# A decoder trunk on one core: where the operands of the matmuls lie in SBUF, modulo 256 bytes

## The chip, the core and the metric

The kernel runs on one core of one Trainium2 chip. The metric is device time in microseconds, from one execution of the whole program; the median of the runs is compared.

## What is computed

A trunk of two layers works on 256 tokens of 1024 channels, in float32. Cut to what matters:

```python
for l in range(2):
    h = h + 0.5 * rmsnorm(swiglu(rmsnorm(h, g[0]), w_gu[l, 0], w_down[l, 0]), g[1])   # FFN, width 2816
    z = rmsnorm(h, g[2]) @ w_in[l]                     # 1024 -> 9224 columns
    y_m = mlstm(conv(z_qk), z_v, z_i, z_f) * sigmoid(z_o)
    y_s = spatial_gating(gelu(z_u), gelu(z_sv), ...)
    y_x = cross_attention(z_xq, rmsnorm(mem, g[6]) @ w_mkv[l])
    merged = sum(sigmoid(z_g)[b] * (y_b @ w_branch[l, b]) for b, y_b in enumerate((y_m, y_s, y_x)))
    h = h + rmsnorm(merged @ w_out[l], g[3])
    h = h + 0.5 * rmsnorm(swiglu(rmsnorm(h, g[4]), w_gu[l, 1], w_down[l, 1]), g[5])
```

## The kernel before, in words

Every large product is done with float32 operands split in two, a high part rounded to the type fp32r and a low part that is the rest; a product is then three matmuls, high by high, high by low, low by high (`product`, L180 to 186, and `rows_mm`, L198 to 205). A matmul has a stationary operand, which a load of its own puts into the array (the profile's PEld), and a moving operand, which streams through (in the profile's `out<-in` the moving operand is named first). Two shapes carry nearly all of the work.

- **256 columns** (L185): the stationary operand is a 128x128 block of a weight, the moving operand one of the eight 256-token rows of an activation. This is `pair_T`: 48 matmuls make 256 output channels. It does the gate and up projections of the FFNs (`o<-xh,hi`, `o<-xh,lo`, `o<-xl,hi`), most of w_in, the three branch projections (`yxh`, `yxl`, `ymh`, `yml`, `ysh`, `ysl`), and the keys of the memory (`mh`, `ml`). Also of this shape are the scores of the cross-attention (`so_<-kT,qx`, the queries stationary) and `attend` (`o<-pT,vx`, the values stationary).
- **512 columns** (L203 to 205): the stationary operand is a 128x128 block of an activation, the moving operand 512 columns of a weight. This is the down projection of the FFNs (`acc<-hi,hh`), the value and spatial parts of w_in (`o<-hi,xh`), the values of the memory (`o<-hi,mh`) and w_out (`acc<-hi,mth`).

One FFN runs over 11 steps; a step is two `pair_T` (96 matmuls of 256 columns) and then, for two slices of the step before, 24 matmuls of 512 columns. A mixer layer is a chain of such groups with short pieces of softmax, scan and normalisation between them. Weights come through a ring: SP issues a DMA into `raw` (4 buffers), ScalarE casts it to `hi` (6 buffers, L114), VectorE subtracts to give `lo` (6 buffers, L115). The order of work on each engine is that of the program text, with a few explicit "issue after" edges (`behind`); the change touches none of them.

Where a tile lies is set by the order of the text. Pools follow one another (`const`, `stream`, `act`, `tmp`, `small`), inside a pool the tags stand in the order of their first use, each at the size of its largest tile times its number of buffers, rounded up to 32 bytes. The first pool starts at byte 16512 of each partition. Summing the sizes gives these starts, modulo 256: `raw`, `hi`, `lo` and all tiles of the tags `t2` and `cv` 192; `xh` 192 and `xl` 0, `qk` 64, `vm` 128, `kT` 192, `ymh` 192, `vx` 0, `yml` 0, `yxh` 64, `yxl` 128. Inside these, `placed` (L118) makes an activation 64 bytes wider than needed and starts it at a given element: 8 (32 bytes) for most, 0 for `mth` and `mtl`, and a value for each of the six FFNs and mixers for `xh` and `xl` (`X_AT`, L37). Every other step inside these operands is a multiple of 512 bytes (blocks of a weight) or 1024 bytes (rows of an activation), so a pair of tiles has one distance modulo 256 for all of its matmuls.

The distance of a pair, moving minus stationary, modulo 256, comes out so (the first number is for the high part of the activation, the second for the low part):

```
256 columns                       moving - stationary
FFN 0 of layer 0   X_AT 4           16,  80
mixer of layer 0   X_AT 8           32,  96
FFN 1 of layer 0   X_AT 12          48, 112
FFN 0 of layer 1   X_AT 2            8,  72
mixer of layer 1   X_AT 6           24,  88
FFN 1 of layer 1   X_AT 10          40, 104
branches: ym 32, 96   ys 160, 224   yx 160, 224      memory keys (mh, ml): 160, 224
scores (kT, qx): 0                attend (pT, vx): 192
512 columns
FFN down (hi or lo with hh, hl): 0
w_in, layer 0: 224, 160    w_in, layer 1: 232, 168
memory values: 96, 32      w_out: 128, 64
```

Of the kernel before, what the change touches and what calls it, by code (L numbers as in the profile page):

```python
# [8 lines left out]
F32 = mybir.dt.float32  # L9
F32R = mybir.dt.float32r  # L10
# [4 lines left out]
P = 128  # L15
D = 1024
KT = D // P
S = 256
NT = S // P
DEPTH = 2  # L20
NH = 4
DQK = 128
DV = 256
# [9 lines left out]
FREE = 4  # L33
BARE_TAIL = 3
BARE_FREE = 3
LINE = 16
X_AT = {(0, 0): 4, (0, 2): 8, (0, 4): 12, (1, 0): 2, (1, 2): 6, (1, 4): 10}  # L37
C_QK, C_V, C_O, C_I, C_F, C_U, C_SV, C_XQ, C_G = 0, 1024, 2048, 3072, 3076, 3080, 4104, 5128, 6152


# [1 line left out]
def decoder_trunk(ctx: ExitStack, tc: tile.TileContext, x, mem, norm_g, w_ffn_gu, w_ffn_down, w_in, conv_w,  # L42
# [4 lines left out]
    const = ctx.enter_context(tc.tile_pool(name="const", bufs=1))  # L47
    stream = ctx.enter_context(tc.tile_pool(name="stream", bufs=4))
    act = ctx.enter_context(tc.tile_pool(name="act", bufs=1))
    tmp = ctx.enter_context(tc.tile_pool(name="tmp", bufs=2))  # L50
# [2 lines left out]
    psa = ctx.enter_context(tc.tile_pool(name="psa", bufs=4, space=bass.MemoryType.PSUM))  # L53

    h = const.tile([P, NT, D], F32, name="h")
    rowA = tmp.tile([112, P], F32, name="rowA", tag="cv", bufs=3)
    nc.scalar.dma_start(rowA, norm_g.rearrange("l n (k p) -> (l n k) p", p=P))
    for tt in range(NT):
# [19 lines left out]
    nc.gpsimd.tensor_copy(sel, sel_f)  # L78
    ones = const.tile([P, P], F32, name="ones")
    nc.gpsimd.memset(ones, 1.0)  # L80
    mhalf = const.tile([P, LINE], F32, name="mhalf")[:, 0:1]
    nc.gpsimd.memset(mhalf, -0.5)
    junk = const.tile([P, 512], mybir.dt.bfloat16, name="junk")
    colA = const.tile([P, 112], F32, name="colA")
    colB = const.tile([P, P], F32, name="colB")
    mgh = const.tile([P, 16], F32, name="mgh")
    def load_consts(src, dst, n):
        pt = ps.tile([P, 512], F32, name="pt", tag="mm")
        nc.tensor.transpose(out=pt[:, :n], in_=src, identity=ident[:n, :n])
        nc.vector.tensor_copy(dst, pt[:, :n])  # L90

    def g_col(l, n, k):
        i = (l * 7 + n) * 8 + k
        return colA[:, i:i + 1]
# [20 lines left out]
            nc.vector.tensor_tensor(out=lo, in0=raw, in1=hi.bitcast(F32), op=ALU.subtract)  # L115
        return hi, lo

    def placed(name, tag, at):  # L118
        t = act.tile([P, KT * S + LINE], F32R, name=name, tag=tag)
        return t[:, at:at + KT * S].rearrange("p (k s) -> p k s", s=S)  # L120

    def load_cols(w, c0, n):
        his, los = [], []
# [41 lines left out]
    def scaled_split(src, gain, hi, lo):  # L165
        last["act"] = nc.scalar.mul(hi, src, gain)  # L166
        last["dve"] = nc.vector.scalar_tensor_tensor(out=lo, in0=src, scalar=gain, in1=hi.bitcast(F32), op0=ALU.mult,  # L167
                                       op1=ALU.subtract)

    def split(src, hi, lo):  # L170
        nc.scalar.copy(hi, src)  # L171
        nc.vector.tensor_tensor(out=lo, in0=src, in1=hi.bitcast(F32), op=ALU.subtract)  # L172

    def split_x(l, n, pts):
        xh, xl = (placed(name, name, X_AT[l, n]) for name in ("xh", "xl"))
        for kt in range(KT):
            scaled_split(pts[kt // 2][:, kt % 2, :], g_col(l, n, kt), xh[:, kt, :], xl[:, kt, :])
        return xh, xl
# [12 lines left out]
    def pair_T(w, c0, xt):  # L191
        wt = load_cols(w, c0, 2 * P)
        o = ps.tile([P, 2, S], F32, name="o", tag="mm")
        for m in range(2):
            cols_T(o[:, m, :], wt, m * P, xt)
        return o
# [10 lines left out]
    def group_rows(w, c0, xt, qs=range(4), os_=None):  # L207
        os_ = os_ or [ps.tile([P, 512], F32, name="o", tag="mm") for _ in range(NT)]
        for q in qs:
            wt = load_rows(w, q * 2 * P, 2, c0, 512)  # L210
            for k in range(2):
                kt = 2 * q + k
                for tt in range(NT):
                    rows_mm(os_[tt], xt, kt, tt, wt, k, 0, kt == 0, kt == KT - 1)
        return os_
# [19 lines left out]
    def boundary(accs, gb, mul, nxt, fill=(), lead=0):  # L235
# [28 lines left out]
        if lead:  # L264
            pts = new_pts()
            for tt in range(NT):
                transpose_in(xs[tt], tt, pts)
        xt = split_x(*nxt, pts)
        if not lead:
            hold[:] = [[]] * BARE_FREE + [[last["act"], last["dve"]]]  # L270
# [63 lines left out]
    kv = {}  # L334

    def kv_parts(l):
        def start():
            mh, ml = placed("mh", "qk", 8), placed("ml", "vm", 8)
            for kt in range(KT):
                scaled_split(memT[:, kt, :], g_col(l, 6, kt), mh[:, kt, :], ml[:, kt, :])  # L340
            kv[l] = ((mh, ml), [act.tile([P, KT, S], F32R, name="kT", tag=t) for t in ("kT", "ymh")],
                     [act.tile([P, NT, D], F32R, name="vx", tag=t) for t in ("vx", "yml")])

        def k_part(c):
            mt, kT, vx = kv[l]
            o = pair_T(w_mkv[l], c * 2 * P, mt)
            split(o, kT[0][:, 2 * c:2 * c + 2, :], kT[1][:, 2 * c:2 * c + 2, :])

        os_ = {}

        def v_quarter(c, q):
            mt, kT, vx = kv[l]
            os_[c] = group_rows(w_mkv[l], D + c * 512, mt, (q,), os_.get(c))
            if q == 3:
                for tt, o in enumerate(os_[c]):
                    split(o, vx[0][:, tt, c * 512:(c + 1) * 512], vx[1][:, tt, c * 512:(c + 1) * 512])

        return start, ([lambda c=c: k_part(c) for c in range(4)] +
                       [lambda c=c, q=q: v_quarter(c, q) for c in range(2) for q in range(4)])

    def mixer(l, xt, nxt, start=None, fill=(), lead=0):
# [20 lines left out]
        wsT = tmp.tile([P, 4, P], F32, name="wsT", tag="wsT", bufs=1)  # L382
        for g in range(4):
            nc.vector.tensor_tensor(out=wsT[:, g, :], in0=wsp[:, g, :], in1=upper, op=ALU.mult)
        yx = placed("yxh", "yxh", 8), placed("yxl", "yxl", 8)
        sc = DH ** -0.5

        _, kT, vx = kv[l]
# [34 lines left out]
            sl = slice(2 * hd, 2 * hd + 2)  # L423
            split(o, yx[0][:, sl, :], yx[1][:, sl, :])

        vm = act.tile([P, NT, NH, DV + 1], F32, name="vm", tag="vm")
        nc.gpsimd.memset(vm[:, :, :, DV:DV + 1], 1.0)

        def proj_v(c):
# [68 lines left out]
        qk = act.tile([P, KT, S], F32, name="qk", tag="qk")  # L498
# [36 lines left out]
                nc.vector.scalar_tensor_tensor(out=mt[1][:, sl, :], in0=mg[:, sl, :], scalar=0.5,  # L535
                                               in1=mt[0][:, sl, :].bitcast(F32), op0=ALU.mult, op1=ALU.subtract)

        ym = placed("ymh", "ymh", 8), placed("yml", "yml", 8)

        def out_gate(hd):  # L540
            so = tmp.tile([P, 2, S], F32, name="so", tag="t2", bufs=T2)
# [71 lines left out]
            gated(c, yr, so)  # L613

        vn = act.tile([P, NT, D], F32, name="vn", tag="vx")
        ys = placed("ysh", "qk", 8), placed("ysl", "vm", 8)
        for c in range(2):
            for tt, o in enumerate(group_rows(w, C_SV + c * 512, xt)):
                nc.scalar.activation(vn[:, tt, c * 512:(c + 1) * 512], o, AF.Gelu_apprx_tanh)
# [17 lines left out]
        def sgu(g):  # L637
            uT = tmp.tile([P, 2, S], F32, name="uT", tag="t2", bufs=T2)
            nc.scalar.activation(uT, pair_T(w, C_U + g * 2 * P, xt), AF.Gelu_apprx_tanh)
            mx = psa.tile([P, 2, NT, P], F32, name="mx", tag="acc")  # L640
            rb = tmp.tile([P, 2, P], F32, name="rb", tag="cv", bufs=3)
            for m in range(2):
                f = 2 * g + m
                for c in range(NT):
                    nc.tensor.matmul(mx[:, m, c, :], vn[:, c, f * P:(f + 1) * P], wsT[:, g, :], start=True,  # L645
                                     stop=True)
            yf = tmp.tile([P, 2, S], F32, name="yf", tag="t2", bufs=T2)
            for m in range(2):
                f = 2 * g + m
                nc.vector.scalar_tensor_tensor(out=rb[:, m, :], in0=rw[:, g, :], scalar=b_col(112 + l * 8 + f),  # L650
                                               in1=bs[:, g, :], op0=ALU.mult, op1=ALU.add)
                nc.vector.scalar_tensor_tensor(
                    out=yf[:, m, :].rearrange("p (c t) -> p c t", c=NT), in0=mx[:, m], scalar=b_col(96 + l * 8 + f),
                    in1=rb[:, m:m + 1, :].to_broadcast([P, NT, P]), op0=ALU.mult, op1=ALU.add)
            sl = slice(2 * g, 2 * g + 2)
            nc.vector.tensor_tensor(out=yf, in0=yf, in1=uT, op=ALU.mult)
            split(yf, ys[0][:, sl, :], ys[1][:, sl, :])
# [3 lines left out]
        for c in range(4):  # L661
            branch(1, 0, ym, c, gate(0, c))
            sgu(c)
        mt = placed("mth", "yxh", 0), placed("mtl", "yxl", 0)
        for c in range(4):
            branch(2, 1, ys, c, gate(1, c), mt)
        if start:
# [16 lines left out]
    transpose_in(xs, 1, pts)  # L684
    load_consts(rowA, colA, 112)
    xt = split_x(0, 0, pts)
    hold[:] = [[first], [], [last["act"], last["dve"]]]
    xt = ffn(0, 0, xt, (0, 2), {2: load_mem, 4: transpose_mem, 6: start0}, kv0, 3)
    xt = mixer(0, xt, (0, 4), start1, kv1[:3], 2)
    xt = ffn(0, 1, xt, (1, 0), {}, kv1[3:8], 3)  # L690
    xt = ffn(1, 0, xt, (1, 2), {}, kv1[8:], 3)
    xt = mixer(1, xt, (1, 4))
    ffn(1, 1, xt, None)

# [26 lines left out]
```

## Time and profile before

| | |
|---|---|
| median of 3 runs | 1532.0 us (1531.25 to 1532.78) |
| the profiled execution | 1531.97 us, span of its instructions 1530.3 us |
| TensorE matmuls busy | 1511.3 us, 99% |
| TensorE weight loads busy | 1425.0 us, 93% |
| VectorE, ScalarE, GpSimd busy | 930.2, 749.6, 44.7 us |
| matmuls | 10870 |
| mean granted TensorE clock | 0.997 |

A matmul's record (281 to 284 ns for 256 columns in the page's list) is its way through the array, and records of neighbours overlap. What a matmul costs in a stream is the distance from one start or end to the next. It is read here from the chain of work that ended last, where a piece `x96` is 96 matmuls in a row with the time that they took together, and from the starts in the timeline.

### The profile page before, as it was taken

The numbers are of one execution on the slowest core, as the hardware profiler recorded it, in microseconds if no ns is written. First come the engines' busy times: TensorE is split into PE (matmuls) and PEld (weight loads), VectorE is DVE, ScalarE is ACT, GpSimd is POOL, SyncE is SP. The second block draws the span as 40 slices with busy tenths as digits, with TensorE's granted clock in tenths as the row PEclk, the third lists the DMA queues.
The fourth block names the chain that finished last, engine by engine and source line by source line (L and its number), as shares of the span: only waits on it lengthen the run. The fifth ranks groups of instructions, "written<-read, shape, count | busy, mean of one in ns | idle before, by whom it ended". The sixth has DMA issues, their size and how long they took to land.

```text
span 1530.3 us, 26328 instructions
## 1 busy us (share of the span) xinstructions
PE 1511.3 (99%) x10870; PEld 1425.0 (93%) x10870; DVE 930.2 (61%) x1319; ACT 749.6 (49%) x972; POOL 44.7 (3%) x77
## 2 busy tenths in 40 slices
PE   7999999999999999999999999999999999899998
PEld 7999998899999999999989999899998999799997
DVE  5564485786765567555475544676877655555444
ACT  6554464554344456444464444565544444454442
POOL 1000000000010000000000000000001000000000
PEclk9999999999999999999999999999999999999999
DMA  8666666455566665656556666655555565476652
GB/s 267 214 182 187 188 193 193 128 161 153 163 183 185 178 192 183 193 182 198 184 178 200 195 185 190 173 158 163 165 151 171 176 180 178 124 220 183 189 180 83
DMA packets 222169, 273.49 MB, mean 179 GB/s; under 512 B 12656, under 2 KB 194144, under 8 KB 222048
## 3 DMA queue, kind: packets, MB, share of 16 engines
q1 hardware_dynamic: 221920, 271.75, 59.2%
q8 instruction: 85, 1.39, 0.4%
q14 instruction: 36, 0.29, 0.1%
q10 hardware_dynamic: 128, 0.06, 0.0%
HBM read 270.72 MB, written 1.05 MB: 178 GB/s over the span
## 4 chain that ended last, share of the span: by engine, by line
PE 96%; DVE 1%; POOL 1%; DMA 0%; ACT 0%; issue 0%; SPq 0%; POOLq 0%; DVEq 0%; ACTq 0%
PE o L185 66%; PE acc L205 6%; PE acc L203 6%; PE acc L204 6%; PE o L203 3%; PE o L205 3%; PE o L204 3%; PE pts L159 1%; DMA raw<-in_w_ffn_gu_dram 0%; PE mx L645 0%; DVE lo L115 0%; PE zif L185 0%; POOL rs L142 0%; POOL rs L591 0%; DVE h L249 0%
## 5 line engine op out<-in xcount | busy, mean ns | idle before, releaser
L115 DVE TENSOR_TENSOR lo<-raw,hi 128x1024 fp32r<-128x1024 f32 x504 | 614.3, 1223 | 507.6 <-ACT hi L114 503.7
L114 ACT CAST hi<-raw 128x1024 fp32r<-128x1024 f32 x504 | 527.6, 1050 | 619.2 <-PE o L185 287.0
L185 PE MATMUL o<-xh,hi 128*128 128x256 f32 x2304 | 653.1, 284 | 1.2 <-ACT xh L166 1.1
L185 PE MATMUL o<-xl,hi 128*128 128x256 f32 x2304 | 651.0, 283 | 0.2 <-DVE xl L167 0.2
L185 PE MATMUL o<-xh,lo 128*128 128x256 f32 x2304 | 647.8, 281 | 0.0
L185 PEld LDWEIGHTS o<-xh,hi 128*128 128x128 f32 x2304 | 438.0, 190 | 3.8 <-ACT xh L166 1.9
L185 PEld LDWEIGHTS o<-xl,hi 128*128 128x128 f32 x2304 | 436.5, 189 | 2.5 <-DVE xl L167 0.8
L185 PEld LDWEIGHTS o<-xh,lo 128*128 128x128 f32 x2304 | 436.8, 190 | 0.1
L205 PE MATMUL acc<-hi,hl 128*128 128x512 f32 x352 | 137.4, 391 | 0.0
L204 PE MATMUL acc<-lo,hh 128*128 128x512 f32 x352 | 137.3, 390 | 0.0
L203 PE MATMUL acc<-hi,hh 128*128 128x512 f32 x352 | 137.1, 390 | 0.0
L205 PEld LDWEIGHTS acc<-hi,hl 128*128 128x128 f32 x352 | 66.0, 188 | 14.2 <-DVE hl L172 0.2
L203 PEld LDWEIGHTS acc<-hi,hh 128*128 128x128 f32 x352 | 66.2, 188 | 12.9 <-ACT hh L171 0.3
L204 PEld LDWEIGHTS acc<-lo,hh 128*128 128x128 f32 x352 | 66.1, 188 | 12.7
L203 PE MATMUL o<-hi,xh 128*128 128x512 f32 x128 | 50.7, 396 | 0.0
L204 PE MATMUL o<-lo,xh 128*128 128x512 f32 x128 | 50.4, 394 | 0.0
L205 PE MATMUL o<-hi,xl 128*128 128x512 f32 x128 | 50.4, 393 | 0.0
L142 POOL TENSOR_TENSOR rs<-ms,mhalf 128x1 f32<-128x1 f32 x26 | 16.3, 628 | 1068.6 <-DVE ms L139 1068.6
L171 ACT CAST hh<-hf 128x512 fp32r<-128x512 f32 x44 | 27.4, 622 | 26.6 <-DVE hf L289 26.6
L185 PE MATMUL o<-yxh,hi 128*128 128x256 f32 x128 | 36.7, 287 | 0.0
L185 PE MATMUL o<-ml,hi 128*128 128x256 f32 x128 | 36.3, 283 | 0.0
L185 PE MATMUL o<-yxl,hi 128*128 128x256 f32 x128 | 36.2, 283 | 0.0
(240 smaller groups left out, 1711.6 us busy)
## 6 DMA issues: line engine op xcount, KB each, us to landing
raw<-in_w_ffn_gu_dram SPq DMA_DIRECT2D x176, 512.0 KB, 4.6
raw<-in_w_in_dram SPq DMA_DIRECT2D x144, 512.0 KB, 3.7
raw<-in_w_ffn_down_dram SPq DMA_DIRECT2D x88, 512.0 KB, 4.4
raw<-in_w_branch_dram SPq DMA_DIRECT2D x48, 512.0 KB, 3.6
raw<-in_w_mkv_dram SPq DMA_DIRECT2D x32, 512.0 KB, 4.6
raw<-in_w_out_dram SPq DMA_DIRECT2D x16, 512.0 KB, 4.3
gb<-in_norm_g_dram SPq DMA_DIRECT2D x6, 512.0 KB, 4.4
h<-in_x_dram SPq DMA_DIRECT2D x4, 256.0 KB, 3.4
```

What stands on the lines that cost most here:

```text
L114: nc.scalar.copy(hi, raw)
L115: nc.vector.tensor_tensor(out=lo, in0=raw, in1=hi.bitcast(F32), op=ALU.subtract)
L142: nc.gpsimd.tensor_tensor(out=rs, in0=ms, in1=mhalf, op=ALU.pow)
L159: nc.tensor.transpose(out=pts[kt // 2][:, kt % 2, tt * P:(tt + 1) * P], in_=xs[kt // 4][:, kt % 4 * P:(kt % 4 + 1) * P], identity=ident)
L171: nc.scalar.copy(hi, src)
L185: nc.tensor.matmul(o, u, v, start=(i == 0), stop=(i == n - 1))
L203: nc.tensor.matmul(o, a, u, start=first, stop=False)
L204: nc.tensor.matmul(o, a, v, start=False, stop=False)
L205: nc.tensor.matmul(o, b, u, start=False, stop=last)
```

## The change

No instruction is added or taken away. The tiles are placed otherwise:

- `X_AT` and the fixed offset of 8 go; `placed` makes a tile as wide as its tag's entry in `TAGS` (in elements of 4 bytes) and starts at 0, but for `yxl` (48 elements, 192 bytes), `yml` (32, 128 bytes) and `mth` (16, 64 bytes).
- `colA` moves from the `const` pool to the head of `act`; `mgh` moves from `const` to the head of `tmp`.
- In `start`, the tiles of the tags `vx` and `yml` are made before those of `kT` and `ymh`, so the order of the tags in `act` is that of `TAGS`.

```diff
-LINE = 16
-X_AT = {(0, 0): 4, (0, 2): 8, (0, 4): 12, (1, 0): 2, (1, 2): 6, (1, 4): 10}
+TAGS = {"xh": 2048, "xl": 2048, "qk": 2048, "vm": 2080, "vx": 2048, "yml": 2080, "kT": 2048, "ymh": 2048,
+        "yxh": 2064, "yxl": 2096}
...
     h = const.tile([P, NT, D], F32, name="h")
+    mgh = tmp.tile([P, 16], F32, name="mgh", bufs=1)
...
-    colA = const.tile([P, 112], F32, name="colA")
+    colA = act.tile([P, 112], F32, name="colA")
     colB = const.tile([P, P], F32, name="colB")
-    mgh = const.tile([P, 16], F32, name="mgh")
...
-    def placed(name, tag, at):
-        t = act.tile([P, KT * S + LINE], F32R, name=name, tag=tag)
-        return t[:, at:at + KT * S].rearrange("p (k s) -> p k s", s=S)
+    def placed(name, tag, dtype=F32R, at=0, n=KT * S):
+        t = act.tile([P, TAGS[tag]], dtype, name=name, tag=tag)
+        return t[:, at:at + n].rearrange("p (k s) -> p k s", s=S)
...
-        xh, xl = (placed(name, name, X_AT[l, n]) for name in ("xh", "xl"))
+        xh, xl = placed("xh", "xh"), placed("xl", "xl")
...
-            mh, ml = placed("mh", "qk", 8), placed("ml", "vm", 8)
+            mh, ml = placed("mh", "qk"), placed("ml", "vm")
...
-            kv[l] = ((mh, ml), [act.tile([P, KT, S], F32R, name="kT", tag=t) for t in ("kT", "ymh")],
-                     [act.tile([P, NT, D], F32R, name="vx", tag=t) for t in ("vx", "yml")])
+            vx = [act.tile([P, TAGS[t]], F32R, name="vx", tag=t)[:, 0:NT * D].rearrange("p (t d) -> p t d", d=D)
+                  for t in ("vx", "yml")]
+            kv[l] = ((mh, ml), [placed("kT", t) for t in ("kT", "ymh")], vx)
...
-        yx = placed("yxh", "yxh", 8), placed("yxl", "yxl", 8)
+        yx = placed("yxh", "yxh"), placed("yxl", "yxl", at=48)
...
-        ym = placed("ymh", "ymh", 8), placed("yml", "yml", 8)
+        ym = placed("ymh", "ymh"), placed("yml", "yml", at=32)
...
-        ys = placed("ysh", "qk", 8), placed("ysl", "vm", 8)
+        ys = placed("ysh", "qk"), placed("ysl", "vm")
...
-        mt = placed("mth", "yxh", 0), placed("mtl", "yxl", 0)
+        mt = placed("mth", "yxh", at=16), placed("mtl", "yxl")
```

Summing the sizes as above: without `colA` (448 bytes) and `mgh` (64) `const` ends 512 bytes earlier, so `raw`, `hi` and `lo` start at 192 as before. `act` begins at 192 with `colA`, so `xh`, `xl`, `qk`, `vm` start at 128; `vm` is 8320 bytes, so `vx` and `yml` start at 0; `yml` is 8320 bytes, so `kT`, `ymh`, `yxh` start at 128; `yxh` is 8256 bytes, so `yxl` starts at 192. `tmp` begins at 128 with `mgh`, and `cv`, `t2` and all behind them lie at the same bytes as before.

## Rows read from the trace of the kernel before

**Rows 1.** The page: engines, granted clock by slice, the chain that ended last.
```profile
span 1530.3 us, 26328 instructions
PE 1511.3 (99%) x10870; PEld 1425.0 (93%) x10870; DVE 930.2 (61%) x1319; ACT 749.6 (49%) x972; POOL 44.7 (3%) x77
...
PEclk9999999999999999999999999999999999999999
...
PE 96%; DVE 1%; POOL 1%; DMA 0%; ACT 0%; issue 0%; SPq 0%; POOLq 0%; DVEq 0%; ACTq 0%
```
**Rows 2.** Timeline near 100 us: start us, us, engine, line, op, names, shape, count.
```profile
100.04 0.28 PE L185 MATMUL o<-xh,lo 128*128 128x256 f32 x1
100.05 0.19 PEld L185 LDWEIGHTS o<-xh,hi 128*128 128x128 f32 x1
100.16 0.28 PE L185 MATMUL o<-xh,hi 128*128 128x256 f32 x1
```
**Rows 3.** The chain in order of time: start us, us, what, count.
```profile
43.31 11.40 PE o L185 x96
60.20 11.40 PE o L185 x96
...
202.81 17.06 PE o L185 x144
...
316.53 24.01 PE o L185 x204
...
473.48 16.96 PE o L185 x144
...
509.19 45.36 PE o L185 x384
...
640.64 11.32 PE o L185 x96
...
827.21 11.35 PE o L185 x96
...
1204.87 17.17 PE o L185 x144
...
1259.07 45.70 PE o L185 x384
...
1364.83 11.60 PE o L185 x96
```
**Rows 4.** Busy time by stretch: us, engines (count), granted clock, DMA share, GB/s.
```profile
43.31:54.71 11.40, 11.40 (x98) 11.40 (x97) 4.44 (x6) 7.46 (x14) 1.10 (x2) 1.00 0.68 219
...
827.21:838.56 11.35, 11.35 (x98) 11.35 (x97) 4.04 (x4) 4.77 (x6) 0.00 (x0) 1.00 0.63 198
1364.83:1376.43 11.60, 11.60 (x98) 11.60 (x97) 4.09 (x4) 4.78 (x6) 0.00 (x0) 1.00 0.62 192
...
307.08:308.33 1.25, 1.25 (x12) 1.24 (x11) 0.00 (x0) 1.15 (x3) 0.00 (x0) 1.00 0.41 59
```
**Rows 5.** Timeline of TensorE near 307 us: one head of `attend`, its last matmul, the next transposes.
```profile
307.08 1.53 PE L185 MATMUL o<-pT,vx 128*128 128x256 f32 x12
...
308.33 0.28 PE L185 MATMUL o<-pT,vx 128*128 128x256 f32 x1
308.45 0.49 PE L411 MATMUL pt<-ident,pr 128*128 128x128 f32 x3
```
**Rows 6.** The chain, 280 to 293 us: scores, then values of w_in, layer 0.
```profile
280.00 1.19 PE so__2977 L185 x10
281.19 0.23 PE o L203
...
292.33 0.69 PE o L185 x6
```
**Rows 7.** The chain, 227 to 251 us and 554 to 577 us: memory values, then w_out.
```profile
226.97 0.35 PE o L185 x3
...
249.72 0.44 PE wsp L381 x4
...
553.95 0.59 PE o L185 x5
...
576.94 11.39 PE o L185 x96
```
**Rows 8.** Who waited for whom: us in total, times, longest us.
```profile
ACT hi L114 <- PE o L185: 287.0, 247, 4.6
...
ACT hi L114 <- PE acc L205: 105.5, 85, 1.9
...
ACT hi L114 <- DMA raw<-in_w_ffn_gu_dram: 14.5, 10, 2.8
```

More of the change, by code (lines that the diff above doesn't have):

```diff
@@ L80, in decoder_trunk @@
     nc.gpsimd.memset(ones, 1.0)
-    mhalf = const.tile([P, LINE], F32, name="mhalf")[:, 0:1]
+    mhalf = const.tile([P, 16], F32, name="mhalf")[:, 0:1]
     nc.gpsimd.memset(mhalf, -0.5)
     junk = const.tile([P, 512], mybir.dt.bfloat16, name="junk")
-    colA = const.tile([P, 112], F32, name="colA")
+    colA = act.tile([P, 112], F32, name="colA")
     colB = const.tile([P, P], F32, name="colB")
-    mgh = const.tile([P, 16], F32, name="mgh")
     def load_consts(src, dst, n):
@@ L424, in attend @@
             split(o, yx[0][:, sl, :], yx[1][:, sl, :])
-        vm = act.tile([P, NT, NH, DV + 1], F32, name="vm", tag="vm")
+        vm = act.tile([P, TAGS["vm"]], F32, name="vm", tag="vm")[:, 0:NT * NH * (DV + 1)].rearrange(
+            "p (t h d) -> p t h d", t=NT, h=NH)
         nc.gpsimd.memset(vm[:, :, :, DV:DV + 1], 1.0)
```

## The prediction

> **What bounds the kernel now.** I read the page first. TensorE's matmuls are busy for 99% of the span, its weight loads for 93%, and the chain that ended last is 96% TensorE, at a granted clock of nine tenths or more in every slice [rows 1]. So what counts is the pace of matmuls in a stream, not waits. That pace is not in the record of one matmul (0.28 us), since records overlap: the next starts after 0.12 us [rows 2]. The same rows show that the load of the following stationary operand starts with each matmul, so two reads of SBUF run at any time, a moving and a stationary one.
>
> The chain gives the pace by stage [rows 3]. A run of 96 matmuls of 256 columns takes 11.40 us in the first FFN (118.8 ns each), 11.32 in the second (117.9), 11.35 in the third (118.2) and 11.60 in the fourth (120.8). In the mixers 144 take 16.96 us (layer 0, 117.8) and 17.17 (layer 1, 119.2), 384 take 45.36 (118.1) and 45.70 (119.0); the keys of the memory 17.06 for 144 (118.5). Shape, count and source line are the same, and the stretches I looked at have the full clock and no gap: the first, third and fourth FFN all show clock 1.00, with TensorE busy for the whole stretch [rows 4]. Within one FFN all steps take the same time (43.31 and 60.20, both 11.40) [rows 3]. What differs from stage to stage, by the table above, is where the activation starts against the weight modulo 256. The 2.5% between the second FFN and the fourth I therefore put down to place.
>
> One group of the same shape is faster still. `attend` starts its 12 matmuls at 307.08, the last of them at 308.33: 1.25 us for 11 steps, 113.6 ns each; with the hand-over to the transposes at 308.45 it is 1.37 for 12, 114.2 [rows 5]. Its clock is 1.00 like the others' [rows 4]. Its distance is 192, the only one of its kind in this kernel, and 192 is what the change gives to all.
>
> **What the change does, part by part.** From the places worked out above: every moving activation (`xh`, `xl`, `mh`, `ml`, `kT`, `ymh`, `yml`, `yxh`, `yxl`, `ysh`, `ysl`) comes to 128, against weights or queries at 192, which is 192 past them. For `attend` nothing changes (192 against 0). In the 512-column shape the FFN's down projection stays at 0, w_out goes from 128 and 64 to 0, and the parts of w_in and the memory values go to 64 (192 against 128), so these do not come to equal places.
>
> The sum, with 113.6 ns for 256 columns. (1) FFNs: 96 matmuls would take 10.91 us; against 11.40, 11.32, 11.35 and 11.60 that is 0.49, 0.41, 0.44 and 0.69, together 2.03 a step, times 11 steps: 22.3 us. (2) Mixers: per layer 1344 matmuls on `xh`, `xl` (28 pairs of 48) and 576 on the branches (12 pairs), 1920; layer 0 runs at about 118.0, layer 1 at about 119.1, so 4.4 and 5.5 ns each: 8.4 and 10.6 us. (3) Keys of the memory: 8 pairs, 384 times 4.9 ns: 1.9 us. (4) Scores: 96 matmuls, now 1.19 us for ten [rows 6], 5.4 ns each: 0.5 us. Together 43.7 us.
>
> 512 columns. The memory values take from 227.32 (226.97 and 0.35) to 249.72, 22.40 us for 96 matmuls, 233.3 ns; w_out takes from 554.54 to 576.94, again 22.40 for 96 [rows 7]. The values of w_in take from 281.19 to 292.33 for 48, 232.1 ns [rows 6]. The FFN's down projection, at distance 0, takes from 54.71 to 60.20 for 24, 228.8 ns [rows 3]. So w_out, 192 matmuls in all, gains 4.5 ns each, 0.9 us. The 576 that go to 64 have no row at 64 alone. The bounds: as slow as the slowest now (233.3), which costs the 384 of w_in some 1.2 ns each, 0.5 us; as fast as distance 0, which gains 3.3 to 4.5 ns on 576, 2.1 us. I take 1 ns, 0.6 us, since w_out has a third of its matmuls at 64 and is no faster for it.
>
> Sum: 43.7 + 0.9 + 0.6 = 45.2 us. The profiled execution took 1531.97 us against a median of 1532.0, so the two may stand for each other: 1532.0 - 45.2 = 1486.8 us.
>
> Costed at nothing: the move of `colA` and `mgh`, which are read by other engines as before; the new order of four tags, since each tile keeps its tag, its buffers and so its waits; the same bytes for `raw`, `hi`, `lo` modulo 256 and for all of `tmp`. No instruction, wait or DMA is added, moved or taken away.
>
> What is next: weights must now come 3% faster. ScalarE's casts already wait 392 us in total for TensorE to give buffers back (287.0 and 105.5), and 14.5 us for FFN weights to land [rows 8]. That is a supply held back by its consumer, so the cover is there; without it the gain of (1) would be lost.
>
> A rule speaks against all of this. The rows above show one shape at one clock with paces from 113.6 to 120.8 ns. The Trainium skill, SBUF — State Buffer, section "Who interferes with whom", gives TensorE one read port for the moving operand and an independent one for the loads, and says "PE and ACT never wait on anyone."; TensorE: Matmul & The Clock Gate, section "Step-by-step: what each phase is for", has it that a load takes no read bandwidth from a running matmul. By that rule place is free and the time stays at 1532; the trace so far does not agree with it.
>
> **The rivals.** *Place does nothing* (first rival): the differences by stage come from something else, say the engines that write beside it, and `attend` is fast because it is short. Then the time is 1532. Against it: the four FFNs do the same work beside the same writers, and step after step repeats to 0.01 us. For it: 113.6 rests on few matmuls, all in `attend`.
>
> *The distance counts modulo more than 256* (second, the slower side). `attend` has its tiles 192 apart modulo 512. The new `xh` starts at 105088 and the first `hi` at 55488: 192 modulo 256, but 448 modulo 512, a distance that no pair of this kernel has. Against it: the `ym` branch lies at 288 modulo 512 and the `xh` of layer 0 at 32, and the two go at one pace: 16.96 for 144, of which 48 are `ym`, is 117.8 ns, and 24.01 for 204, of which 12 are `attend` (1.37) and the rest `xh` and `xl`, leaves 117.9 [rows 3]. If it counts all the same, the pace may be anything between the rows. At the worst, 120.8 ns, 8544 matmuls (all but `attend`) lose about 2 ns on the mean of 118.7: 1532 + 18 = 1550. It ends slower from a pace of 118.9 on. If it is instead the best of the others, 117.9, the gain is 8 us, 1524.
>
> *The supply becomes the bound* (third): the FFN's steps keep their 16.89 us (43.31 to 60.20) and only the rest gains, 1532 - 22.9 = 1509. Against it: rows 8, and 219 GB/s in a stretch of an FFN where another ran with 192 [rows 4].
>
> **How the numbers follow.** The forecast has 0.79; within it 113.0 ns (the resolution of 0.01 us at both ends of the 11 steps) to 114.2, and the bounds of the 512 columns, give 1480 to 1493. Place does nothing: 0.04. Modulo more than 256: 0.05 for slower, 0.06 for a small gain. Supply: 0.06. The range takes the forecast and the nearer half of the supply's case, up to 1500, which also covers a pace of 115 (1499); about 0.82 lies inside. Faster by over 0.2%, about what a measurement of this kernel can tell from no change: 0.79 + 0.06 + 0.06 = 0.91; same 0.04; slower 0.05.
>
> **What would show it.** The pieces of 96 matmuls should come to 10.9 us in all four FFNs alike, those of 144 to 16.4, those of 384 to 43.6; the down projection should keep 5.49 us for 24, and a step should come to 16.4 us. `attend` should not change; w_out should come from 22.40 to 22.0. If 96 matmuls stay at 11.3 to 11.6 and differ by stage, the first rival holds; if they are alike but over 11.2, the second; if they are 10.9 with gaps behind DMA or casts, the third. The prediction is wrong above all if 192 is good only for the places that `attend` has.

## The result and the profile after

The changed kernel takes 1513.26 us (median of 4 runs, 1511.53 to 1514.27) against 1532.39 for the kernel before in the same comparison. The ratio is 0.9874, 95% interval 0.9857 to 0.9891: 19 us faster. The direction was as forecast, the size was not: 45.2 us were forecast, and 1513 lies above the range, which ended at 1500.

The page of the changed kernel, to be read against [rows 1]:

```profile
span 1512.5 us, 26330 instructions
PE 1493.2 (99%) x10870; PEld 1410.2 (93%) x10870; DVE 929.3 (61%) x1319; ACT 749.0 (50%) x972; POOL 44.6 (3%) x77
...
PEclk9999999999999999999999999999999999999999
...
PE 96%; DVE 2%; POOL 1%; DMA 0%; ACT 0%; issue 0%; SPq 0%; POOLq 0%; DVEq 0%; ACTq 0%
```

Nothing but TensorE's busy time moved: the same 10870 matmuls at the same granted clock, still 96% of the chain. So the pace of the streams has changed, less than forecast. The chain in order of time says where (start us, us, what, count), against [rows 3]:

```profile
60.89 11.31 PE o L185 x96
77.64 11.31 PE o L185 x96
96.24 11.13 PE o L185 x96
...
315.20 23.21 PE o L185 x204
434.30 16.34 PE o L185 x144
451.54 16.96 PE o L185 x144
...
505.10 45.23 PE o L185 x384
...
652.36 11.31 PE o L185 x96
...
837.44 11.31 PE o L185 x96
...
1246.50 45.23 PE o L185 x384
...
1366.68 11.31 PE o L185 x96
```

The steps behind a down projection now run alike in all four FFNs, as forecast, but at 11.31 us for 96 (117.8 ns), not 10.91. And two groups stand out that do run at the forecast pace: 16.34 us for 144 at 434.30 is 113.5 ns, while the next 144, of the same kinds and at the same distances, take 16.96 (117.8). The step at 96.24, which follows transposes instead of a down projection, takes 11.13 with its entrance. In the kernel before, the step at that point took 11.62 where its neighbours took 11.40:

```profile
95.83 11.62 PE o L185 x96
112.94 11.40 PE o L185 x96
```

So an entrance from transposes costs 0.22, and the 96 themselves go at 10.91. At one distance, 192, the same shape has two paces, 113.3 and 117.8 ns from start to start, and no long stream settles between them. `attend`, whose own distance the change leaves at 192, shows it too: its two heads of layer 0 that follow 256-column matmuls (from 313.19 and 320.50) take 1.42 and 1.41 us for 12 where they took 1.38.

w_out goes further than forecast (22.0 us): it runs from 550.32 (548.91 and 1.41) to 572.08, 21.76 us for 96, 226.7 ns, where it took 22.40 [rows 7].

```profile
548.91 1.41 PE o L185 x12
...
572.08 0.94 PE o L185 x8
```

Summed over both traces from start to start, with a matmul that waited counted at the pace of its stream, the 17.8 us of span come from: 256 columns on `xh` and `xl` -12.7 (FFNs -7.0, mixers -5.7), branches -2.7, down projection -1.3, w_out -1.3, values of w_in -0.8, all the rest of the 512 and 256 columns -0.5; waits behind transposes and at the start of the program +1.7, which differ by up to 2.4 us between the runs below.

### The profile page after: what moved, and what is told of

Same layout as the page of the kernel before. It is cut to its first block, busy times and chain, and to the rows that moved or that the text cites. A ratio compares the mean times of both kernels' runs of the same rounds, so it can differ in the third digit from the quotient of the medians.

```text
span 1512.5 us, 26330 instructions
## 1 busy us (share of the span) xinstructions
PE 1493.2 (99%) x10870; PEld 1410.2 (93%) x10870; DVE 929.3 (61%) x1319; ACT 749.0 (50%) x972; POOL 44.6 (3%) x77
## 4 chain that ended last, share of the span: by engine, by line
PE 96%; DVE 2%; POOL 1%; DMA 0%; ACT 0%; issue 0%; SPq 0%; POOLq 0%; DVEq 0%; ACTq 0%
PE o L185 65%; PE acc L203 6%; PE acc L205 6%; PE acc L204 6%; PE o L203 3%; PE o L205 3%; PE o L204 3%; PE pts L159 1%; DMA raw<-in_w_ffn_gu_dram 0%; PE mx L647 0%; DVE lo L115 0%; PE zif L185 0%; POOL rs L142 0%; POOL rs L593 0%; ACT xh L166 0%
## 5 line engine op out<-in xcount | busy, mean ns | idle before, releaser
L185 PE MATMUL o<-mh,hi 128*128 128x256 f32 x128 | 36.1, 282 | 0.0
L185 PE MATMUL o<-mh,lo 128*128 128x256 f32 x128 | 36.0, 281 | 0.0
```

The source lines that it names most:

```text
L185: nc.tensor.matmul(o, u, v, start=(i == 0), stop=(i == n - 1))
```

## The experiments

The theory after the result, A: at one distance a stream of matmuls has more than one steady pace, and what comes ahead of it picks one. In the trace after, all 96-matmul steps behind a down projection (distance 0) are slow, the groups of 48 and 144 behind w_in's values (distance 64) fast; one head of `attend` behind the same values, at 1032.29, is slow. The rivals: B, the slow pace belongs to the FFN stages, to what the other engines do there; C, for the third experiment on, anything additional at that point shifts the stream. In every run the weights lie at 192. So 0 and 64 for what comes ahead always mean a stationary operand at 192 or at 128, and these runs cannot tell the distance from that place alone; for the stream itself `attend`, with its tiles at 192 and 0, has the same two paces as `xh` and the weights at 128 and 192.

**Down projection at another distance.** One 64-byte tile is made later, so that the tiles of `hh` and `hl` start at 128 and the down projection has 64 instead of 0.

```diff
     h = const.tile([P, NT, D], F32, name="h")
-    mgh = tmp.tile([P, 16], F32, name="mgh", bufs=1)
...
     nc.gpsimd.tensor_copy(sel, sel_f)
+    mgh = tmp.tile([P, 16], F32, name="mgh", bufs=1)
```

> One 64-byte tile (mgh) moves behind the tags cv and t2, so that these start at 128 instead of 192. The FFN's down projection then has a distance of 64 instead of 0; pairs of w_in, the branches and the memory keys stay at 192. In the changed kernel the streams of 256 columns at distance 192 have two paces, 113.3 and 117.8 ns, and those that follow 512-column matmuls at distance 0 have the slower one, those that follow a distance of 64 mostly the faster one. Theory A (at one distance there are two steady paces; what comes ahead of a stream picks one): 96 matmuls in the FFNs go from 11.31 to about 10.90 us, 40 times, -16 us; the 24 down matmuls go from 5.44 to about 5.53, +4 us; attend (now 128) and the scores (now 0) lose about 1 us: about 1500 us. Theory B (the slower pace belongs to the FFN stages themselves, to what the other engines do there): 96 stay at 11.31, the down projection costs 4 us more: about 1518 us.

Measured: 1500.89 us (1498.49 to 1502.61), ratio to the kernel before 0.9793, interval 0.9777 to 0.981. The chain:

```profile
60.44 10.91 PE o L185 x96
95.09 11.54 PE o L185 x96
...
465.33 16.96 PE o L185 x144
...
647.75 10.91 PE o L185 x96
...
831.33 10.91 PE o L185 x96
...
1389.03 10.91 PE o L185 x96
```

The FFN steps are at 10.91 us, in all four FFNs, with `xh` and the weights where they were: A, and B has fallen. The step behind transposes went the other way, from 11.13 to 11.54 (11.32 without its entrance): the transposes read tiles that moved too. The mixer's groups behind 128-column matmuls (`mx`, the spatial gating) stay at 16.96.

**One matmul more, at distance 64.** All places as in the changed kernel; ahead of each FFN step from the third on, one more 512-column matmul, whose result is written over.

```diff
-    def pair_T(w, c0, xt):
+    def pair_T(w, c0, xt, first=False):
         wt = load_cols(w, c0, 2 * P)
         o = ps.tile([P, 2, S], F32, name="o", tag="mm")
+        if first:
+            nc.tensor.matmul(o.rearrange("p m s -> p (m s)"), xt[0][:, 0, 0:P],
+                             last["hi"][:, 0:2, :].rearrange("p k c -> p (k c)"), start=True, stop=True)
...
-            pa = pair_T(w, j * 2 * P, xt)
+            pa = pair_T(w, j * 2 * P, xt, j > 1)
```

(`last["hi"]` is the first `hi` of the pair.)

> All places as in the changed kernel. Ahead of the first product of each FFN step from the third on, one more matmul of 512 columns is done at distance 64 (a block of xh stationary, two rows of hi moving); its result is written over by the product that follows. 36 such matmuls cost about 0.23 us each, 8 us. Theory A: one matmul at the other distance is enough to change the pace of the 96 behind it, to 10.90 us, -15 us: about 1506 us; or one is too few to change it, then 1521 us and nothing is decided. Theory B: 1521 us, all at 11.31.

Measured: 1507.61 us in one run. Lines have shifted by one: `product` is L186 here (L188 in the runs with other distances), and the additional matmul is L196. The chain:

```profile
59.12 0.23 PE o L196
59.35 10.90 PE o L186 x96
```

36 matmuls that do nothing useful make the kernel 6 us faster.

**The control: one matmul more, at distance 0.** The same, with a block of `hi` stationary.

```diff
-            nc.tensor.matmul(o.rearrange("p m s -> p (m s)"), xt[0][:, 0, 0:P],
+            nc.tensor.matmul(o.rearrange("p m s -> p (m s)"), last["hi"][:, 2, 0:P],
```

> The control for the run with one more matmul of 512 columns ahead of each FFN step from the third on: the same matmul, but with a block of hi stationary instead of one of xh, so that its distance is 0 and not 64. Theory A (the distance of what comes ahead picks the pace): the 96 behind it stay at 11.31 us, 36 matmuls at 0.23 us come on top, 8 us: about 1521 us. Rival C (any additional matmul there, whatever its place, shifts the stream into the faster pace): 10.9 us for 96, about 1507 us.

Measured: 1521.39 us in one run, as A says; C has fallen. The chain:

```profile
60.96 11.31 PE o L186 x96
77.93 1.18 PE o L186 x10
...
96.54 0.46 PE o L196
97.00 10.91 PE o L186 x96
```

The step behind transposes (97.00) kept the fast pace through the one matmul at distance 0. So a single one does not make a stream slow; the 24 of a down projection at 0 do, each time.

**The same matmul in the kernel with the down projection at 64.**

```diff
-    mgh = tmp.tile([P, 16], F32, name="mgh", bufs=1)
...
+    mgh = tmp.tile([P, 16], F32, name="mgh", bufs=1)
...
+            nc.tensor.matmul(o.rearrange("p m s -> p (m s)"), last["hi"][:, 2, 0:P],
+                             last["hi"][:, 0:2, :].rearrange("p k c -> p (k c)"), start=True, stop=True)
```

> The kernel whose FFN down projection stands at distance 64 (about 1501 us, 96 matmuls in 10.91 us), with the additional matmul at distance 0 ahead of each step from the third on. Theory A, if one matmul is enough in this direction too: 96 go back to 11.31 us, +14 us, and the additional matmuls cost 8 us: about 1523 us. If one at distance 0 is too few, or rival C holds: 96 stay at 10.91, about 1509 us.

Measured: 1518.1 us in one run, between the two. One step of each FFN in the chain, in order, and for the second and third FFN what precedes their first down projection:

```profile
60.62 10.90 PE o L186 x96
...
582.34 28.27 PE o L186 x240
...
633.57 11.31 PE o L186 x96
...
796.87 19.54 PE o L186 x170
...
838.76 10.90 PE o L186 x96
...
1367.78 11.31 PE o L186 x96
```

Neither expectation: two FFNs are fast in all their steps behind the matmul, two slow, with the same code and the same places. The trace shows what differs: the two fast FFNs begin fast (the 192 matmuls ahead of the first down projection go at 113.3 ns once past their waits; 19.54 us for 170 in the third FFN has such waits in it), the slow ones begin slow (28.27 for 240 is 117.8). With this sequence ahead of a step, neither pace is forced, and a stream keeps the one it had, through 24 down matmuls and the additional one, step after step. That is what two steady paces would do, and no theory with one pace for each place can.

**Other distances.** `xh` and `xl` are put into one tile 256 bytes wider, at a place of its own for each FFN and mixer; two small tags lose one of four buffers to make room.

```diff
+X_AT = {(0, 0): 60, (0, 2): 48, (0, 4): 4, (1, 0): 8, (1, 2): 12, (1, 4): 56}
...
-        xh, xl = placed("xh", "xh"), placed("xl", "xl")
+        at = X_AT[l, n]
+        x2 = act.tile([P, 2 * KT * S + 64], F32R, name="xh", tag="xh")
+        xh, xl = (x2[:, o:o + KT * S].rearrange("p (k s) -> p k s", s=S) for o in (at, at + KT * S))
...
-                mv4 = small.tile([P, 2, 2], F32, name="mv4", tag="mv4")
+                mv4 = small.tile([P, 2, 2], F32, name="mv4", tag="mv4", bufs=3)
...
-                r4 = small.tile([P, 2], F32, name="r4", tag="r4")
+                r4 = small.tile([P, 2], F32, name="r4", tag="r4", bufs=3)
```

> xh and xl of each FFN and mixer are placed at a distance of their own (both the same): FFNs at 176, 208, 224, 160 in order, mixers at 128 and 240; all else as in the changed kernel. Theory A says that 192 is one of several distances with more than one steady pace: some FFN stages show two kinds of steps (the first, which is entered from transposes, another than those entered from the down projection), with 96 between 10.9 and 11.6 us. Theory B: each stage has one pace of its own, 11.3 or more at all distances. If a distance near 192 has 10.9 in all steps, that is the place to take.

One step of each FFN (two of the first), at 176, 208, 224 and 160 (1521.72 us in all):

```profile
60.53 11.44 PE o L188 x96
77.46 11.44 PE o L188 x96
...
639.62 11.44 PE o L188 x96
...
843.64 11.36 PE o L188 x96
...
1373.21 11.39 PE o L188 x96
```

At 176, 208 and 224 each FFN has one pace, in the steps that follow a down projection and in those that do not. At 160 the two kinds of steps that A suggested do show, closer together than at 192: from start to start the 192 matmuls ahead of the first down projection go at 117.2 to 117.6 ns, the steps behind it at 118.5 to 119.0.

> The same with the FFNs at 0, 64, 128, 96 and the mixers at 32 and 112. The kernel before had xh and xl 64 apart at 8 to 48 and gave 11.32 to 11.60 us for 96; here both have one distance. If the distance of each pair alone sets the pace, 0 to 128 give 11.3 to 11.6 us for 96; nothing below 11.2 is expected by either theory.

With the FFNs at 0, 64, 128 and 96 and the mixers at 32 and 112 (`X_AT` 16, 24, 32, 48, 44 and 40 in the order of the line above; 1519.43 us in all):

```profile
61.36 11.51 PE o L188 x96
...
637.77 11.31 PE o L188 x96
...
841.20 11.52 PE o L188 x96
...
1215.42 16.44 PE o L188 x144
...
1369.82 11.52 PE o L188 x96
```

The FFN at 128 again has two kinds: 118.3 to 118.8 ns ahead of the first down projection, 119.8 to 120.0 behind it. And here is what neither theory expected: the mixer of layer 1, at 112, takes 16.44 us for 144 behind 128-column matmuls, where 192 takes 16.96. From start to start its matmuls on `xh` settle at 113.3 within the first 24, behind transposes, 257-column and 512-column matmuls alike.

> As the other two scans, with the FFNs at 112, 120, 104, 116 and the mixers at 184 and 200, to see how wide the fast places are. If 112 is a narrow place, 104 and 120 (8 bytes off) are slow and 116 is between; if it is wide, all four FFNs are near 10.9 us for 96. At 184 and 200, 8 bytes off 192, streams behind transposes tell whether 192's two paces are there as well.

FFNs at 112, 120, 104 and 116, mixers at 184 and 200 (1529.5 us in all):

```profile
60.02 10.92 PE o L188 x96
...
636.01 11.57 PE o L188 x96
...
841.68 11.54 PE o L188 x96
...
1378.87 11.69 PE o L188 x96
```

112 is fast behind a down projection at 0 as well, and it is a narrow place: 4 bytes off it is the slowest of all (121.8 ns), 8 bytes off little better.

**All FFNs and mixers at 112.** The same edit with 44 for all six.

> xh and xl in one tile, both at distance 112 from the weights in all FFNs and mixers; all else as in the changed kernel (the down projection at 0, branches and memory keys at 192). At 112 the mixer of layer 1 ran at 113.4 to 114.3 ns whatever came ahead: transposes, 257-column matmuls, 128-column matmuls. Theory A1 (112 has a fast pace alone): 96 matmuls of an FFN step take 10.9 us behind a down projection at 0 too, -16 us; w_in and the branches behind it gain about 10 us: about 1487 us. Theory A2 (112 has a slow pace as well, and a down projection at 0 picks it, as it does at 192): 96 stay at 11.3 or more, only the mixers gain: about 1503 us.

Measured: 1491.77 us (1491.33 to 1493.18), ratio to the kernel before 0.9736, interval 0.972 to 0.9753. The chain:

```profile
60.30 10.92 PE o L188 x96
...
94.94 11.14 PE o L188 x96
...
198.92 16.96 PE o L188 x144
...
465.09 16.44 PE o L188 x144
...
499.76 43.81 PE o L188 x384
...
627.71 10.92 PE o L188 x96
```

A1: at 112 a stream comes to the fast pace from every entrance in this kernel. In the trace it takes some nine matmuls, most of them at 116 to 121 ns, to get there behind a down projection, then it stays at 113.3. The 16.96 at 198.92 are the memory keys, which were left at 192 behind a down projection at 0. The changed kernel has the same 16.96 there, though the wider tile of `xh` moves the keys' activation by 256 bytes: for them a whole 256 changes nothing. Against the 1487 expected, 5 us are missing. From start to start, against the changed kernel: the streams on `xh` and the branches gained 24.2 us and not 26, in part for the slow matmuls at each entrance; the values of w_in lost 1.4, since `xh` is their stationary operand and its move took them from 64 to 144; the down projection lost 1.1 and waits 0.7.

## Why the prediction was wrong, point by point

- **What bounds the kernel**: right. TensorE's pace sets the time, before and after, and all that moved is that pace.
- **Place sets the pace**: right in part, and the first rival has fallen; but at 192 place alone does not set it. w_out is the plainest case: its shape and work unchanged, 22.40 to 21.76 us, and 21.76 to 21.78 in all the later runs, whatever the pace of the streams ahead of it. The prediction read the rule of the Trainium skill (SBUF — State Buffer, "Who interferes with whom") as saying that place is free; that does not hold for these streams: the runs have 113.3 to 121.8 ns for one shape at one granted clock.
- **113.6 ns for distance 192**: this is the step that failed. The number was right for the 12 matmuls it was read from; that it belongs to the distance was not shown by them. The head in [rows 5] followed 512-column matmuls of w_in's values (160 and 224), the others the same or 256-column matmuls of w_in at distances of 24 to 96; none followed a down projection at 0 or the 128-column matmuls, which stand ahead of most streams. So the rows held a few kinds of entrance, and not those that count. What the runs showed in its place: at 192 a stream goes at 113.3 or at 117.8 ns, and what comes ahead of it picks which; the FFN steps came to 11.31 us behind a down projection at 0 and to 10.91 behind one at 64. With it terms (1) to (4) were mis-sized together: 22.3 us for the FFNs became 7.0 (0.09, 0.01, 0.04 and 0.29 us for a step behind a down projection; five of the other nine steps ran at the fast pace), and the 21.4 us of the mixers, keys and scores came to 8.9.
- **512 columns**: w_out gained 1.3 us against 0.9 (226.7 ns, under the 228.8 that it was given); w_in and the memory values 1.0 us against 0.6, inside their bounds. The down projection, which was to keep its 5.49, gained 1.3 us: 24 matmuls take 5.44 us (72.20 to 77.64). Its distance is not the reason, and the streams beside it matter: in the run with `xh` at 176, with the down projection still at 0, it takes 5.49 again (71.97 to 77.46).
- **The second rival**, a distance that counts modulo more than 256, was given 0.11 and the signature "alike but over 11.2". The signature came, the rival is not the cause: `xh` at one place, 448 modulo 512 from the weights, has both paces in one trace (11.31 and 10.91 for 96). It was a signature that another cause could write as well.
- **Supply**: right. With 40 us taken out in the last experiment the FFN steps still show no gap.
- What was missing among the rivals was that the neighbour work could set the pace. The prediction's last sentence, that 192 may be good only for the places that `attend` has, came nearest, though it is the entrance that counts. The forecast of 1486.8 us was 5 us from what the last experiment reached (1491.77), but at another distance; that 112 has the same fast pace as 192, and from every entrance tried, was not foreseen, so the nearness is in part luck.

What stays open: why a stream at one distance settles at two paces, why 112 showed only one, which part of a preceding stream does the picking, and whether it is its distance or the place of its stationary operand alone. The traces show the two paces and that they last; they do not show the reads themselves.

## What to carry to other kernels

In a stream of matmuls with a weight load each, read the pace from start to start by stage, and look for distances between moving and stationary operand modulo 256 bytes that run faster; here 7% lay between the best and the worst. Before a pace is carried from one stage to another, ask what stood ahead of it in each: take it only where the entrances are alike, or try an entrance of the other kind. A place that is fast from every entrance tried (112 here) is worth more than one that is fast from some.

## What the runs showed of the hardware that was not expected

- One shape, one pair of places, one granted clock: 96 matmuls of an FFN step in 10.91 or in 11.31 us behind a down projection, with nothing between, and a stream of 384 behind 128-column matmuls that keeps the slow one to its end (45.23 us for 384).
- 36 additional matmuls of 0.23 us, whose results are thrown away, made the kernel 6 us faster (1513.26 to 1507.61), and the same 36 at another distance 8 us slower (1521.39).
- The pace can be inherited over many steps, through the down projections between them: in one run two of four equal FFNs were fast throughout and two slow.
- 4 bytes of place are worth 0.77 us in 96 matmuls (10.92 at distance 112, 11.69 at 116, in two FFNs of one run).
